# A scheduler's order: evictions of convolved tiles and splits of weight columns given an earlier rank

## The chip, the cores and the metric

The kernel runs on one core of one Trainium2 chip. A core has TensorE (matrix products, written to PSUM banks), VectorE, ScalarE and GpSimd (element-wise work), SyncE (which here only issues DMA transfers), and 16 DMA engines; each engine works through its own queue of instructions, and the engines wait for each other on semaphores. The metric is the device time of one execution in microseconds (us), lower is better.

## The reference

The reference is a two-layer trunk of a diffusion model on 512 latent and 256 context tokens of width 1024, in float32. Layer 0 mixes the tokens with a gated delta rule, layer 1 with retention; each mixer is followed by a feed-forward of width 4096 with squared ReLU. Cut to what matters here:

```python
proj = jnp.concatenate([hc, hl], axis=1) @ w_in            # 768 tokens x 6208 columns
qkv = jnp.concatenate([silu(short_conv(qkv[:, :n_ctx], conv_w)),
                       silu(short_conv(qkv[:, n_ctx:], conv_w))], axis=1)
...
# chunked_linear_attention, for each head and direction, over chunks of tokens
dec = jnp.where(incl, jnp.exp(jnp.where(incl, seg, 0.0)), 0.0)
qk = jnp.einsum('bhncd,bhnsd->bhncs', q, k) * dec
a = jnp.where(strict, jnp.einsum('bhncd,bhnsd->bhncs', k, k) * dec * beta[..., :, None], 0.0)
sol = lax.linalg.triangular_solve(a + jnp.eye(CHUNK, dtype=f32), rhs, ...)
...
def step(s, xs_n):
    un = un - jnp.einsum('bhcd,bhde->bhce', xs_n[5], s)
    o = jnp.einsum('bhcd,bhde->bhce', qd, s) + jnp.einsum('bhcs,bhse->bhce', qkn, un)
    s = s * gt[..., None, None] + jnp.einsum('bhcd,bhce->bhde', kd, un)
```

The short convolution has four taps, along the tokens, for each column on its own. There are 8 query/key heads of 128 and 16 value heads; one query/key head serves two value heads.

## The kernel before, in words

**Products in two parts.** Each float32 product is made as three products of rounded operands: a matrix is split into a rounded part and a remainder (`split`, lines 56 and 57: a ScalarE copy that rounds, then a VectorE subtraction). The normalized tokens lie split and transposed in `xt`. Weights come by DMA into `raw` tiles and are split into `hl` tiles, either as 128 columns of all 1024 rows (`w_cols`, lines 64 to 77; in two halves of 512 rows in layer 0's mixer, in one piece later) or as a block of 256 rows by 512 columns (`w_block`). `raw` has two buffers, `hl` has three in layer 0's mixer and five later.

**Projection tiles.** One tile is 128 columns of the input projection for all 768 tokens. `gemm_pair` makes 24 matmuls for the 512 latent tokens (tile `gl`) and then 24 for the 256 context tokens (`gc`), all at line 91. In layer 0's mixer `self.gc` is `("gl", 2)`, so both draw their PSUM bank from one tag of two buffers.

**Convolved tiles.** There are 32 of them, `conv_tile` (lines 572 to 585): two per pair of value heads for key and query, two for the values. The bank is evicted together with the convolution: ScalarE copies it times the tap c[2] into `acc` (line 579), then VectorE adds the other three taps, one instruction each, each on top of the one before (line 582). A Silu on ScalarE (lines 592, 595, 629) takes `acc` further. The 16 gate tiles z (`z_tile`) are evicted by a Silu at line 442 and stored.

**Eight pairs.** For each pair of value heads p the stages are: `gdn_s1` (key and query tile, norms), `gdn_sv` (two value tiles), `gdn_bt` (24 Relu and 24 Exp on ScalarE for the decay, lines 649 and 657), `gdn_s2` (the decay products: on VectorE a mask at line 673, `qkd` at 679 and `e` at 682, then transposes at 691, a transfer of 32x32 blocks through DRAM, and 30 rounds of elimination at lines 717 and 720), `gdn_iv` (assembling the inverse, products at lines 754 to 797), and twelve `gdn_step`s, six chunks in two directions (products at 847, 848, 865, 875, 886; VectorE at 851, 882, 890, 892; ScalarE at 856, 870, 873). `gdn_y2` (lines 915 to 922) transposes the result. The loop over the pairs in `layer0_mix` weaves the steps of pair p with the inverse of pair p+1, the value tiles of p+1, the key and query tiles of p+2, z tiles, and modulation rows (`mod_rows`, lines 220 to 237).

**What sets the order.** The kernel is written for a scheduler that turns the program into one queue for each engine. It runs the program on a clock of its own and, when an engine is free, gives it that one of the ready instructions that has the lowest rank; the rank is the place in the program. `high_priority(n)` moves the rank of what is written inside it forward by n places. The steps stand in a block with `PRI = 300`, the decay products, the inverse and the output parts in one with `P2 = 400`, the key and query tiles and the decay's exponentials in one with `PS = 250`; the value tiles and z tiles have none. The first two weight columns of each feed-forward and the first of the retention have `WP = 200`. The order thus found is fixed: on the chip each engine takes its queue in that order.

**After the mixer** come the output projection (`out0`), the feed-forward (`ffn`), retention (`layer1_mix`) and the second feed-forward. They use `w_cols` too, for the first matrix of the feed-forwards and for retention's queries and keys; their `proj` uses `w_block`.

## Time and profile before

| | |
|---|---|
| median of 3 runs | 2562.77 us (2562.68 to 2563.67) |
| profiled execution, its own time | 2564.44 us |
| its span, first to last instruction | 2562.7 us |
| mean granted TensorE clock | 0.98 |
| busy: TensorE / weight loads / VectorE / ScalarE / GpSimd | 2431.7 / 2010.7 / 1661.7 / 1074.0 / 163.7 us |
| the evictions at line 579 (ScalarE) and line 582 (VectorE) | 22.0 + 15.3 us and 71.6 + 45.6 us |
| splits of weights, 128x512 halves, lines 56 / 57 | 98 each, 60.6 / 67.4 us |

A row of the groups is read as: line, engine, operation, out<-in, shapes, xcount | busy us, mean ns of one | idle time of that engine just before, and what ended most of it. A row of the waits is: engine and line that waited <- engine and line it waited for: us in total, times, longest. A row of a timeline is: start us, us, engine, line, operation, names, count, and in brackets the engine's idle time before it and what ended that. PE is TensorE's matmul, PEld its weight load, DVE VectorE, ACT ScalarE, POOL GpSimd, SPq the queue of SyncE. The granted clock is the share of full speed that TensorE's throttle allowed.

### The profile page before, as it was taken

How to read it: one execution, taken by the hardware profiler on the slowest of the kernel's cores; microseconds unless marked ns; L12 is line 12 of the kernel's file. 1: busy time of each engine (PE TensorE's matmuls, PEld its weight loads, DVE VectorE, ACT ScalarE, POOL GpSimd, SP SyncE). 2: the span in 40 equal slices, each digit the busy share in tenths (PEclk: the TensorE clock that was granted, in tenths of full speed). 3: DMA queues.
4: the chain of work that ended last, by engine and by line, in shares of the span. 5: the costliest groups of instructions: out<-in, count | busy, mean ns of one | idle time of the engine just before them, and what ended most of it. 6: DMA issues, size and time to landing. Idle time of an engine off the chain costs nothing.

```text
span 2562.7 us, 38997 instructions
## 1 busy us (share of the span) xinstructions
PE 2431.7 (95%) x14879; PEld 2010.7 (78%) x14879; DVE 1661.7 (65%) x3382; ACT 1074.0 (42%) x2357; POOL 163.7 (6%) x248
## 2 busy tenths in 40 slices
PE   8799798998888999999999999999999999999998
PEld 4687686786777787878888888888888887788887
DVE  5568767777776845887876667874353546644446
ACT  5576556565654553253222222653231322532222
POOL 1101111111201110000000000000000000000000
PEclk9899899899999999999999999999999999999999
DMA  6332324333132238354444444243122223433332
GB/s 211 89 96 77 106 51 113 80 105 94 43 109 67 74 113 272 132 165 132 132 144 129 123 130 129 100 135 93 50 84 61 78 66 115 150 97 91 107 91 91
DMA packets 346828, 276.94 MB, mean 108 GB/s; under 512 B 105608, under 2 KB 293488, under 8 KB 346640
## 3 DMA queue, kind: packets, MB, share of 16 engines
q1 hardware_dynamic: 345616, 271.30, 35.2%
q10 hardware_dynamic: 1024, 3.15, 0.5%
q8 instruction: 117, 1.92, 0.3%
q14 instruction: 71, 0.58, 0.1%
HBM read 241.72 MB, written 32.67 MB: 107 GB/s over the span
## 4 chain that ended last, share of the span: by engine, by line
PE 58%; DVE 5%; DMA 2%; ACT 2%; issue 1%; POOL 0%; SPq 0%; POOLq 0%; DVEq 0%; ACTq 0%
PE pn L940 22%; PE gl L91 14%; PE rvp L1257 5%; PE gc L91 3%; PE rl L91 3%; PE rgp L1257 3%; PE pv L1287 3%; PE sc L1265 1%; PE rc L91 1%; PE nps L276 1%; DVE hl L57 0%; DVE ma L199 0%; DMA zt<-zd 0%; PE mps L214 0%; PE uo L865 0%
## 5 line engine op out<-in xcount | busy, mean ns | idle before, releaser
L91 PE MATMUL gl<-xt,hl 128*128 128x512 f32 (+2 forms) x2760 | 704.6, 404 | 53.9 <-DVE acc L582 31.9
L91 PEld LDWEIGHTS gl<-xt,hl 128*128 128x128 f32 x2760 | 517.0, 194 | 161.9 <-issue 27.9
L57 DVE TENSOR_TENSOR hl<-raw,hl 128x1024 fp32r<-128x1024 f32 (+1 forms) x306 | 321.4, 1052 | 231.1 <-ACT hl L56 230.3
L56 ACT ACTIVATE hl<-raw 128x1024 fp32r<-128x1024 f32 (+1 forms) x306 | 280.0, 920 | 409.6 <-PE pn L940 251.9
L940 PE MATMUL pn<-hl,fh 128*128 128x512 f32 x1920 | 444.7, 391 | 2.2 <-DVE fh L1074 1.9
L940 PEld LDWEIGHTS pn<-hl,fh 128*128 128x128 f32 x1920 | 357.3, 188 | 80.0 <-DVE fh L1074 5.0
L91 PE MATMUL gc<-xt,hl 128*128 128x256 f32 x1944 | 273.2, 289 | 8.9 <-DVE acc L582 4.7
L91 PEld LDWEIGHTS gc<-xt,hl 128*128 128x128 f32 x1944 | 253.3, 193 | 19.9 <-ACT zs L442 5.5
L199 DVE SCALAR_TENSOR_TENSOR ma<-mraw,cst,ma 128x256 f32<-128x256 f32 x280 | 123.5, 482 | 40.4 <-DMA mraw<-in_w_mod 38.1
L940 PE MATMUL pn<-hl,yh 128*128 128x512 f32 x576 | 133.8, 392 | 2.5 <-ACT yh L56 1.4
L954 DVE TENSOR_TENSOR facc<-pn,facc 128x512 f32<-128x512 f32 x120 | 82.5, 689 | 81.8 <-PE pn L940 81.5
L1257 PE MATMUL rvp<-hl,xt 128*128 128x512 f32 x576 | 132.8, 389 | 0.0
L940 PEld LDWEIGHTS pn<-hl,yh 128*128 128x128 f32 x576 | 107.2, 188 | 26.8 <-ACT yh L56 2.6
L1257 PEld LDWEIGHTS rvp<-hl,xt 128*128 128x128 f32 x576 | 107.8, 188 | 22.2
L1071 ACT ACTIVATE fr<-gl 128x512 f32<-128x512 f32 x64 | 38.2, 597 | 193.3 <-PE gl L91 190.7
L582 DVE SCALAR_TENSOR_TENSOR acc<-gl,cw,acc 128x511 f32<-128x511 f32 (+1 forms) x96 | 71.6, 746 | 37.9 <-ACT acc L579 37.1
L940 PE MATMUL pn<-hl,ryt 128*128 128x512 f32 x384 | 92.0, 397 | 0.0
L1257 PE MATMUL rgp<-hl,xt 128*128 128x512 f32 x384 | 91.0, 393 | 0.0
L91 PE MATMUL rl<-xt,hl 128*128 128x512 f32 x384 | 89.5, 391 | 0.4 <-DVE hl L57 0.4
L717 DVE TENSOR_TENSOR tmp<-u 112x30 f32<-112x30 f32 (+14 forms) x240 | 81.5, 339 | 9.4 <-POOL u L709 6.2
L940 PEld LDWEIGHTS pn<-hl,ryt 128*128 128x128 f32 x384 | 71.6, 188 | 16.8
L91 PEld LDWEIGHTS rl<-xt,hl 128*128 128x128 f32 x384 | 71.5, 188 | 15.7 <-DVE hl L57 0.9
(282 smaller groups left out, 3347.9 us busy)
## 6 DMA issues: line engine op xcount, KB each, us to landing
raw<-in_w_ff SPq DMA_DIRECT2D x128, 512.0 KB
mraw<-in_w_mod SPq DMA_DIRECT2D x112, 256.0 KB
raw<-in_gdn_w_in SPq DMA_DIRECT2D x96, 256.0 KB
raw<-in_ret_w_in SPq DMA_DIRECT2D x32, 512.0 KB
mraw<-in_w_mod SPq DMA_DIRECT2D x24, 512.0 KB
e<-gd SPq DMA_DIRECT2D x32, 384.0 KB
mraw<-in_w_mod SPq DMA_DIRECT2D x8, 1024.0 KB
raw<-in_gdn_w_out SPq DMA_DIRECT2D x16, 512.0 KB
```

What stands on the lines that cost most here:

```text
L56: nc.scalar.activation(out=hi, in_=src, func=AF.Copy)
L57: nc.vector.tensor_tensor(out=lo, in0=src, in1=hi.bitcast(F32), op=ALU.subtract)
L91: nc.tensor.matmul(ps, lhsT=w(a, k), rhs=xt[:, b, k, t0:t0 + n], start=(k == 0 and i == 0), stop=(k == 7 and i == 2))
L199: eng.scalar_tensor_tensor(out=accs[v], in0=raw[:, k], scalar=c, in1=accs[v], op0=ALU.mult, op1=ALU.add)
L276: nc.tensor.transpose(ps[:, k, :], xn[:, (half * 4 + k) * 128:(half * 4 + k + 1) * 128], self.ident)
L582: nc.vector.scalar_tensor_tensor(out=acc[:, t0 + a:t0 + a + m], in0=ps[:, b:b + m], scalar=c[j], in1=acc[:, t0 + a:t0 + a + m], op0=ALU.mu ...
L717: nc.vector.tensor_tensor(out=t3, in0=u3[:, 0:c, c:c + 1].to_broadcast([112, c, n]), in1=u3[:, c:c + 1, c + 1:32].to_broadcast([112, c, n] ...
L940: m = nc.tensor.matmul(ps, lhsT=lhs(a, k, t), rhs=hls[hf][k // 2][:, b, k % 2], start=(k == 0 and n == 0), stop=(k == 3 and n == 2))
L954: nc.vector.tensor_tensor(out=dst, in0=ps, in1=dst, op=ALU.add)
L1071: nc.scalar.activation(out=r, in_=ps, func=AF.Relu)
L1257: nc.tensor.matmul(ps, lhsT=xt[:, a, kk, t * 128:(t + 1) * 128], rhs=hls[kk // 2][:, b, kk % 2], start=(kk == 0 and n == 0), stop=(kk == 7 ...
L1287: nc.tensor.matmul(pvs[it], lhsT=pts[jt][:, i, it * 128:(it + 1) * 128], rhs=v[:, j, jt], start=(jt == 0 and n == 0), stop=(jt == 5 and n ...
```

## The change

A constant `EV = 500` is added. The split in `w_cols` and the whole loop of evictions in `conv_tile` are put into `high_priority(EV)`. The instructions stay the same, with the same operands; only their rank for the scheduler moves, by 500 places, in addition to that of a block around them. The DMA transfer of the weights and the matmuls keep their rank, as do the evictions of z tiles and the splits in `w_block`.

```diff
@@ -30,6 +30,7 @@
 PRI = 300
 PS = 250
 P2 = 400
+EV = 500
@@ -72,7 +73,8 @@
             hl = self.whl.tile([128, 2, n, 128], F32R, tag="hl", name="hl")
-            self.split(hl[:, 0], hl[:, 1], raw)
+            with self.tc.high_priority(EV):
+                self.split(hl[:, 0], hl[:, 1], raw)
             res.append(hl)
@@ -575,13 +577,14 @@
         acc = prep.tile([128, T], F32, tag="acc", name="acc", bufs=2)
-        for ps, t0, n in segs:
-            nc.scalar.activation(out=acc[:, t0:t0 + n], in_=ps, func=AF.Copy, scale=c[2])
-            for j, a, b in ((0, 2, 0), (1, 1, 0), (3, 0, 1)):
-                m = n - max(a, b)
-                nc.vector.scalar_tensor_tensor(
-                    out=acc[:, t0 + a:t0 + a + m], in0=ps[:, b:b + m], scalar=c[j], in1=acc[:, t0 + a:t0 + a + m],
-                    op0=ALU.mult, op1=ALU.add)
+        with self.tc.high_priority(EV):
+            for ps, t0, n in segs:
+                nc.scalar.activation(out=acc[:, t0:t0 + n], in_=ps, func=AF.Copy, scale=c[2])
+                for j, a, b in ((0, 2, 0), (1, 1, 0), (3, 0, 1)):
+                    m = n - max(a, b)
+                    nc.vector.scalar_tensor_tensor(
+                        out=acc[:, t0 + a:t0 + a + m], in0=ps[:, b:b + m], scalar=c[j], in1=acc[:, t0 + a:t0 + a + m],
+                        op0=ALU.mult, op1=ALU.add)
         return acc
```

## Prediction

> **What bounds the kernel now.** I read the page first, then the busy time by stretch, then who waited for whom on TensorE, and last the timeline around the longest wait.

> ```profile
> span 2562.7 us, 38997 instructions
> PE 2431.7 (95%) x14879; PEld 2010.7 (78%) x14879; DVE 1661.7 (65%) x3382; ACT 1074.0 (42%) x2357; POOL 163.7 (6%) x248
> PEclk9899899899999999999999999999999999999999
> 64.00:960.00 896.00, 798.88 (x7109) 667.37 (x7108) 642.27 (x1639) 520.32 (x1430) 127.74 (x184) 0.95 0.32 87
> 960.00:2562.70 1602.70, 1578.10 (x7511) 1313.86 (x7509) 981.90 (x1660) 520.14 (x871) 24.38 (x44) 1.00 0.37 116
> ```

> The last two rows (stretch, then length, PE, PEld, DVE, ACT, POOL busy, granted clock, DMA share, GB/s) divide the kernel. From 960 us on TensorE is idle for 24.6 of 1602.7 us at full clock: there is next to nothing to win. From 64 to 960 us, the gated delta-rule stage, it is idle for 97.1 us and its granted clock is 0.95. Whatever this change gives must come from those 97.1 us and that clock. VectorE is busy for 642 of the 896 us (0.72), ScalarE for 520.

> Who ended TensorE's idle time between 64 and 960 us (waits in total, times, longest):

> ```profile
> PE gl L91 <- DVE acc L582: 31.9, 11, 9.1
> PE yps L921 <- DVE o L915: 6.7, 8, 1.5
> PE ivps L754 <- DVE v L745: 6.3, 3, 5.9
> PE gl L91 <- ACT zs L442: 5.4, 1, 5.4
> PE gl L91 <- DVE hl L57: 5.4, 3, 3.1
> PE gl L91 <- ACT hl L56: 5.1, 3, 4.2
> PE gc L91 <- DVE acc L582: 4.7, 2, 4.2
> ```

> The evictions of convolved tiles (L582) end 36.6 us in 13 waits, the weight splits (L56, L57) 10.5 us in 6. All the rest, 97.1 − 47.1 = 50.0 us, is waits on the recurrence, its inverse, the z evictions (L442) and small rows. In this stage the latent and the context product of a tile alternate on the two buffers of one PSUM tag, so the next tile's product waits for the eviction of the bank before last. The timeline around the longest wait shows what the eviction stood behind:

> ```profile
> 386.89 7.13 ACT L657 ACTIVATE e<-e,lw 128x128 f32<-128x128 f32 x24
> 389.09 3.03 PE L91 MATMUL gc<-xt,hl 128*128 128x256 f32 x24
> ...
> 396.09 0.67 ACT L579 ACTIVATE acc<-gl,cw 128x512 f32<-128x512 f32 x1
> ...
> 400.24 0.69 DVE L679 TENSOR_TENSOR qkd<-qm,e 128x512 f32<-128x512 f32 x1
> ...
> 400.84 0.75 DVE L582 SCALAR_TENSOR_TENSOR acc<-gl,cw,acc 128x511 f32<-128x511 f32 x1
> ...
> 401.73 4.91 PE L91 MATMUL gl<-xt,hl 128*128 128x512 f32 x14 [9.06 <-DVE acc L582]
> ```

> The tile's bank was full when the context product began at 389.09. ScalarE first ran 24 exponentials of the decay (7.13 us), and the eviction's first step came at 396.09; on VectorE its three further steps then took turns with the decay products (L673, L679, L682). TensorE stood for 9.06 us. This is the order that the change turns round.

> **Evictions.** No instruction is added or removed. Of 32 convolved tiles, 64 ScalarE copies and 192 VectorE steps move. Their rank goes ahead by 500, which is more than the 400 of the decay products and the 300 of the steps; for the key and query tiles it adds to a 250 that they have, for the value tiles there was none. Durations, and those of the decay products:

> ```profile
> L582 DVE SCALAR_TENSOR_TENSOR acc<-gl,cw,acc 128x511 f32<-128x511 f32 (+1 forms) x96 | 71.6, 746 | 37.9 <-ACT acc L579 37.1
> L582 DVE SCALAR_TENSOR_TENSOR acc<-gc,cw,acc 128x255 f32<-128x255 f32 (+1 forms) x96 | 45.6, 475 | 1.3 <-ACT acc L579 0.9
> L679 DVE TENSOR_TENSOR qkd<-qm,e 128x512 f32<-128x512 f32 x48 | 35.3, 735 | 15.8 <-ACT e L657 15.2
> L682 DVE TENSOR_TENSOR e<-kkps,e 128x512 f32<-128x512 f32 x48 | 32.9, 686 | 0.7
> L579 ACT ACTIVATE acc<-gl,cw 128x512 f32<-128x512 f32 x32 | 22.0, 688 | 52.3 <-PE gl L91 52.1
> ```

> Served at once, a latent bank is free after 0.688 + 3 × 0.746 = 2.93 us, while its context product (the row at 389.09) takes 3.03 us: no wait. But the three steps depend on each other, and in the timeline another instruction slips between them; with one of 0.735 us between each the bank is free after 5.13 us, a wait of 2.1 us. I take 2.1 × 0.72, the share of time in which VectorE has something else to do: 1.5 us for each of the 13 waits, 20 us left of 36.6, **17 us gained** (bounds 36.6 − 27.3 = 9.3, and 36.6).

> **Splits.** 98 half-tile splits in this stage, and those of the feed-forward and query/key columns later:

> ```profile
> L57 DVE TENSOR_TENSOR hl<-raw,hl 128x512 fp32r<-128x512 f32 x98 | 67.4, 690 | 32.7 <-ACT hl L56 32.4
> L56 ACT ACTIVATE hl<-raw 128x512 fp32r<-128x512 f32 x98 | 60.6, 629 | 40.8 <-PE gc L91 31.3 <-DMA raw<-in_gdn_w_in 6.9 <-DVE tmp L717 2.3
> 716.87 1.08 SPq L72 DMA_DIRECT2D raw<-in_gdn_w_in  x2
> 721.37 0.61 ACT L56 ACTIVATE hl<-raw 128x512 fp32r<-128x512 f32 x1
> PE gl L91 <- ACT hl L56: 4.1, 1, 4.1
> ```

> The 5.4 us in which the VectorE half was late goes, since what stood ahead of it there were decay transposes and small rows. Of the ScalarE half's 5.1 us, the wait of 4.2 us stays: its weights were requested at 716.87, 4.5 us before the split at 721.37, so the transfer was late and not the rank. The last row is the one wait after 960 us, at the start of the first feed-forward; the split there stood behind norm evictions, its transfer may also have been late, and I take half. 5.4 + 0.9 + 2.0: **8 us** (bounds 0 and 14.6). A split issues no transfer, but it frees the raw buffer for which the next load waits on SP's queue, with the block transfers of the inverse and the recurrence's stores behind it there; earlier splits can only shorten that. Later splits cost nothing in the forecast: a five-buffer ring and up to 24.6 us of idle time in all cover them; if a split took a buffer that an output-projection block needs first, TensorE's feed-forward products would be the cover.

> **Clock.** Six stretches at half clock lie at the waits named so far. The second of them, the wait at which it lies, and the sum of the six:

> ```profile
> 500.50:507.30 6.80, 6.16 (x15) 4.79 (x16) 6.67 (x14) 0.85 (x1) 4.05 (x6) 0.50 0.57 126
> 501.14 5.06 PE L91 MATMUL gl<-xt,hl 128*128 128x512 f32 x11 [2.90 <-DVE acc L582]
> sum 37.40, PE 27.15 PEld 21.00 DVE 30.85 ACT 3.61 POOL 15.11; mean PE 4.52 PEld 3.50 DVE 5.14 ACT 0.60 POOL 2.52
> ```

> 27.15 us of TensorE work ran at half speed, so 13.6 us were lost. I give back the share in which the waits go, 25 of 51.2 us: **7 us** (bounds 0 and 13.6).

> [...]

> **What it costs.** Evictions are 71.6 + 45.6 = 117.2 us of VectorE's 642, 18%, now mostly in front of the recurrence's and the inverse's steps. I let the other 50.0 us of TensorE's waits grow by that share: **9 us**. At best 0, since TensorE has projection products of other tiles to run while a step is late; at worst double, 18. A gain in these waits I exclude, because every instruction they hang on has the same or a later place. What stands behind an early eviction is one step at a time, 0.75 us; behind an early split whose weights are late, the whole ScalarE queue: exponentials, the scaled updates, the next eviction.

> **Sum.** 17 + 8 + 7 − 9 = 23 us. The profiled execution took 2564.4 us, 1.7 above its span and 1.7 above the median of 2562.8; a difference between stages carries over to the median unchanged. 2562.8 − 23 = **2540 us**. With the terms at their ends this case runs from about 2518 to 2556.

> **Rivals.** *Decay products late, slower.* The next pair's first step hangs on its decay products, the block transfer, the inverse and its products. If the evictions of two tiles, 2 × 3 × (0.746 + 0.475) = 7.3 us, go ahead of them in each of seven pairs and each chain moves by all of it, that is 51 us against the 32 gained: 2582 us. It decides against the change from 32 / 7 = 4.6 us per pair. Against it, the same stretch one pair from the end:

> ```profile
> 819.41 0.47 DVE L582 SCALAR_TENSOR_TENSOR acc<-gc,cw,acc 128x255 f32<-128x255 f32 x1
> 819.81 0.67 DVE L682 TENSOR_TENSOR e<-kkps,e 128x512 f32<-128x512 f32 x1
> ```

> The last decay product already ends after the last eviction step, so turning round what lies before moves its end little. For it: evictions that are free earlier let the next tile's come earlier too, into the same stretch. Chance 0.16.

> *The pair chain holds the end, no difference.* The stage's last work, from the chain of waits:

> ```profile
> 945.20 0.63 PE yps L921 x4
> 945.83 0.47 PE gl L91 x2
> 946.30 2.88 PE gc L91 x24
> ```

> The last pair's transposes end at 945.8, the last z tile's product at 949.2. If projection tiles come sooner but the pairs' chain does not, only 3.4 us come off: 2559 us, and idle time moves to the end of the stage. The same would be read if the scheduler's own clock, and not the rank, puts the evictions where they are. Against it: the chain itself starts from key and query tiles that TensorE must first make. Chance 0.13.

> *All of it goes.* Evictions and splits wait for nothing, the clock stays up, and the step chain loses nothing: 36.6 + 14.6 + 13.6 = 65 us, 2498 us; it needs VectorE free at each of the 13 moments. Chance 0.06, with most of it short of that end.

> *Splits hold ScalarE, slower.* Seven of the 98 splits were held by a transfer for 6.9 us together, about 1 us each, and one wait of 4.2 us on TensorE came of it. If all 98 stood at the head of the queue like that, 97 us on ScalarE would become 97 × 4.2 / 6.9 = 59 us on TensorE, 36 us more than the gain: 2599 us. [...] Against this rival stand L56's 31.3 us behind context products: mostly a free buffer, not a transfer, gates a split. Chance 0.05.

> **How the numbers follow.** The forecast has 0.60. A measurement of this kernel can tell about 0.2%, 5 us, from no change. Faster is the forecast and the large gain, 0.66; within 0.2% 0.13; slower 0.16 + 0.05 = 0.21. The range goes from 2512, below the forecast's own end, to 2578, which takes in no difference and most of a slow outcome up to its price; about 0.05 lies below and 0.12 above.

> **What would show it.** Right: in the stage, waits on L582 fall from 36.6 to about 20 us with none above 3, waits on the VectorE half of a split vanish, half-clock stretches after 400 us shrink, ScalarE's copy (L579) stands among the exponentials and not behind them, and after 960 us TensorE is idle for about as long as before. Wrong: if waits on L582 fall but idle time in the stage does not, the cost term was too small, and the rows of L754, L865, L875 and L921 will have grown; if the waits on L582 stay, the rank was not the cause; if L56 waits long on transfers, the last rival holds; if the loss lies after 960 us, it is the ring of split buffers.

## The result, and the profile after

The changed kernel takes 2543.1 us (median of 4 runs, 2540.9 to 2548.3) against 2563.2 us before (4 runs, 2562.7 to 2566.7): a ratio of 0.9925, with an interval from 0.9907 to 0.9943. That is 20 us, four times what a measurement of this kernel can tell from no change. The profiled execution was the slowest of the four, 2548.25 us. In e1 and e12 below one execution each ran at a granted clock of 0.84 and took 7% longer; those two times are left out, and so is e12's profile, which is of one of them. All line numbers after the change are 1 to 3 higher: evictions stand at L582 (ScalarE) and L585 (VectorE), splits at L57 and L58, z evictions at L444. In the kernels of the experiments the same lines stand up to two places off.

The page's first lines, the clock, and the busy time of the two parts of the kernel (stretch, length, PE, PEld, DVE, ACT, POOL busy, granted clock, DMA share, GB/s):

```profile
span 2546.6 us, 38986 instructions
PE 2427.1 (95%) x14879; PEld 2007.0 (79%) x14879; DVE 1656.9 (65%) x3382; ACT 1072.3 (42%) x2357; POOL 162.6 (6%) x248
PEclk9899999999999989999999999999999999999999
60.00:928.60 868.60, 795.15 (x7162) 665.80 (x7160) 637.18 (x1641) 524.16 (x1436) 125.93 (x184) 0.96 0.34 92
960.00:2546.60 1586.60, 1551.68 (x7344) 1290.19 (x7343) 967.01 (x1644) 504.40 (x849) 25.07 (x44) 0.99 0.36 110
```

The mixer's end is best read from the first product of the output projection. It begins at 928.6 us, before at 965.7. The same stretch of before, to compare with the fourth row:

```profile
60.00:965.70 905.70, 808.58 (x7163) 675.85 (x7163) 646.35 (x1644) 526.12 (x1436) 127.74 (x184) 0.95 0.32 88
```

So the mixer is 37.1 us shorter: 13.4 us of them because the same products kept TensorE busy for 795.2 in place of 808.6 us, which is the clock (TensorE's work in stretches at half clock falls from 64.6 to 39.1 us, so 12.8 us less are lost there), and 23.7 us because it is idle for 73.4 in place of 97.1 us. But the span is only 16.1 us shorter (the medians differ by 20.1). From the first output-projection product to the end before took 2562.7 − 965.7 = 1597.0 us, after 2546.6 − 928.6 = 1618.0 us. **21.0 us of the gain are given back after the mixer**, where the forecast had nothing.

Who ended TensorE's idle time from 64 to 960 us:

```profile
PE gl L93 <- ACT zs L444: 13.1, 1, 13.1
PE pn L943 <- ACT hl L57: 12.4, 1, 12.4
PE gl L93 <- ACT hl L57: 6.1, 3, 4.0
PE gl L93 <- DVE acc L585: 6.0, 7, 1.4
...
PE gc L93 <- DVE acc L585: 3.4, 2, 3.1
...
PE gc L93 <- ACT zs L444: 2.2, 2, 1.5
```

The waits on the taps fell from 36.6 us in 13 to 9.4 us in 9. In their place stand two single waits of a dozen us each, which are no evictions of convolved tiles. The first is a z tile's, whose evictions the change left where they were:

```profile
100.50 7.12 ACT L660 ACTIVATE e<-e,lw 128x128 f32<-128x128 f32 x24
107.63 1.28 ACT L444 ACT_TABLE_LOAD   x1
108.92 0.60 ACT L444 ACTIVATE zs<-gl 128x512 f32<-128x512 f32 x1
109.42 0.38 ACT L444 ACTIVATE zs<-gc 128x256 f32<-128x256 f32 x1
109.57 4.78 PE L93 MATMUL gl<-xt,hl 128*128 128x512 f32 x13 [13.11 <-ACT zs L444]
```

This is the picture of the long wait before, with Silu in the eviction's place: 24 exponentials and a table load stand ahead of two evictions of 1 us together. The second lies at the mixer's end:

```profile
913.20 3.03 PE L93 MATMUL gc<-xt,hl 128*128 128x256 f32 x24
921.24 0.38 SPq L83 DMA_DIRECT2D raw<-in_gdn_w_out  x1
927.49 1.06 ACT L57 ACTIVATE hl<-raw 128x1024 fp32r<-128x1024 f32 x1 [1.55 <-DMA raw<-in_gdn_w_out]
928.60 2.06 PE L943 MATMUL pn<-hl,yh 128*128 128x512 f32 x3 [12.37 <-ACT hl L57]
```

Before, the products of two more z tiles ran from 949 us on and covered the loads of the first y, z and weight blocks. Now the projection is used up when the last pair is done, and the loads are bare.

What the change does inside the mixer is seen where the exponentials of a pair meet an eviction:

```profile
649.56 0.69 ACT L582 ACTIVATE acc<-gl,cw 128x512 f32<-128x512 f32 x1 [3.09 <-PE gl L93]
...
650.28 0.75 DVE L585 SCALAR_TENSOR_TENSOR acc<-gl,cw,acc 128x510 f32<-128x510 f32 x1 [0.66 <-ACT acc L582]
...
650.95 0.36 DVE L720 TENSOR_TENSOR tmp<-u 112x198 f32<-112x198 f32 x1
...
651.22 0.75 DVE L585 SCALAR_TENSOR_TENSOR acc<-gl,cw,acc 128x511 f32<-128x511 f32 x1
...
652.15 0.74 DVE L585 SCALAR_TENSOR_TENSOR acc<-gl,cw,acc 128x511 f32<-128x511 f32 x1
...
655.98 0.46 ACT L582 ACTIVATE acc<-gc,cw 128x256 f32<-128x256 f32 x1
...
656.34 3.02 ACT L660 ACTIVATE e<-e,lw 128x128 f32<-128x128 f32 x10
```

The latent bank is free at 652.89, 3.33 us after the copy began, with one step of the elimination (0.36 us) between the taps; the context copy cuts into the run of exponentials. TensorE does not wait here at all.

### The profile page after: what moved, and what is told of

It is laid out like the page before. It is cut to its first block, busy times and chain, and to the rows that moved or that the text cites. A ratio compares the mean times of both kernels' runs of the same rounds, so it can differ in the third digit from the quotient of the medians.

```text
span 2546.6 us, 38986 instructions
## 1 busy us (share of the span) xinstructions
PE 2427.1 (95%) x14879; PEld 2007.0 (79%) x14879; DVE 1656.9 (65%) x3382; ACT 1072.3 (42%) x2357; POOL 162.6 (6%) x248
## 4 chain that ended last, share of the span: by engine, by line
PE 65%; DVE 10%; DMA 4%; ACT 3%; issue 2%; POOL 1%; POOLq 0%; SPq 0%; DVEq 0%; ACTq 0%
PE pn L943 21%; PE gl L93 16%; PE rvp L1260 5%; PE gc L93 5%; PE rl L93 3%; PE rgp L1260 3%; PE pv L1290 3%; DMA mraw<-in_w_mod 1%; DVE hl L58 1%; PE sc L1268 1%; DVE ma L201 1%; PE uo L868 1%; PE uo L889 1%; PE kk L878 1%; PE rc L93 1%
## 5 line engine op out<-in xcount | busy, mean ns | idle before, releaser
L93 PE MATMUL gl<-xt,hl 128*128 128x512 f32 (+2 forms) x2760 | 702.9, 400 | 36.5 <-ACT zs L444 13.1
L93 PEld LDWEIGHTS gl<-xt,hl 128*128 128x128 f32 x2760 | 507.2, 191 | 137.5 <-ACT zs L444 13.6
L58 DVE TENSOR_TENSOR hl<-raw,hl 128x1024 fp32r<-128x1024 f32 (+1 forms) x306 | 322.1, 1055 | 241.8 <-ACT hl L57 234.9
L57 ACT ACTIVATE hl<-raw 128x1024 fp32r<-128x1024 f32 (+1 forms) x306 | 280.8, 920 | 440.8 <-PE pn L943 256.3
L943 PE MATMUL pn<-hl,fh 128*128 128x512 f32 x1920 | 449.9, 393 | 4.3 <-DVE fh L1077 3.6
L93 PE MATMUL gc<-xt,hl 128*128 128x256 f32 x1944 | 278.8, 291 | 7.8 <-DVE acc L585 3.4
L943 PE MATMUL pn<-hl,yh 128*128 128x512 f32 x576 | 135.1, 395 | 13.5 <-ACT hl L57 12.4
L93 PEld LDWEIGHTS rl<-xt,hl 128*128 128x128 f32 x384 | 72.6, 191 | 15.3 <-DVE hl L58 0.3
L1260 PEld LDWEIGHTS rgp<-hl,xt 128*128 128x128 f32 x384 | 71.3, 188 | 14.7
L723 DVE TENSOR_TENSOR u<-u,tmp 112x30 f32<-112x30 f32 (+14 forms) x240 | 80.5, 336 | 2.3
```

The costliest lines, as they stand in the source:

```text
L57: nc.scalar.activation(out=hi, in_=src, func=AF.Copy)
L58: nc.vector.tensor_tensor(out=lo, in0=src, in1=hi.bitcast(F32), op=ALU.subtract)
L93: nc.tensor.matmul(ps, lhsT=w(a, k), rhs=xt[:, b, k, t0:t0 + n], start=(k == 0 and i == 0), stop=(k == 7 and i == 2))
L723: nc.vector.tensor_tensor(out=u3[:, 0:c, c + 1:32], in0=u3[:, 0:c, c + 1:32], in1=t3, op=ALU.subtract)
L943: m = nc.tensor.matmul(ps, lhsT=lhs(a, k, t), rhs=hls[hf][k // 2][:, b, k % 2], start=(k == 0 and n == 0), stop=(k == 3 and n == 2))
L1260: nc.tensor.matmul(ps, lhsT=xt[:, a, kk, t * 128:(t + 1) * 128], rhs=hls[kk // 2][:, b, kk % 2], start=(kk == 0 and n == 0), stop=(kk == 7 ...
```

## The experiments

My theory after the result: the evictions carry the mixer's gain, and the raised splits outside the mixer cost what was lost there. Rivals: the splits carry the gain; or the gain is an accident of the new order, as any small move of ranks would throw it about. Each kernel was timed beside the kernel before on the same chip, which had medians of 2560.0 to 2561.7 us there.

**e1: evictions alone.** `high_priority(EV)` stays in `conv_tile` and is taken out of `w_cols`.

> Only the evictions of convolved tiles get the earlier rank; all splits keep theirs. Theory: the evictions carry most of the 37 us by which the first output-projection product comes sooner (965.7 before, 928.6 changed), and the splits outside the mixer cause the 21 us lost after it. Then that product starts at about 935, the part after it takes 1597 as before, and the time is about 2533 us. Rival A, the splits in the mixer carry the gain: about 2555 to 2563. Rival B, the 21 us lost later do not come from splits (any new order of the mixer leaves them): about 2548 to 2552.

2554.4 us, ratio 0.9974 (0.9960 to 0.9988): a miss for the theory, whose 2533 is 21 us away, at the edge of what rival A gave. The waits from 60 to 960 us:

```profile
PE gl L92 <- ACT hl L57: 15.6, 5, 10.6
PE gl L92 <- DVE acc L584: 11.4, 9, 2.5
PE gc L92 <- DVE acc L584: 10.5, 5, 3.5
```

The evictions' waits fall from 36.6 to 21.9 us, but 10 us of that turn up again as waits on the ScalarE half of the splits, which were 5.1. The mixer ends at 954.0 us, 11.7 earlier and not the 31 of the theory; from there to the end it takes 1597.1 us, as before, which is the theory's other half.

**e2: splits alone.** The reverse: in `w_cols` only, for all stages.

> Only the splits of weight columns get the earlier rank, in the mixer and after it; the evictions keep theirs. Theory: at most 8 us come off in the mixer and about 20 are lost after it: 2570 to 2578 us, slower than before, with the waits on evictions still about 36 us. Rival A, splits carry the gain: 2530 to 2545. Rival B, no loss from splits after the mixer: 2553 to 2558.

2590.2 us, 1.0118 (1.0100 to 1.0137), 12 us above the range expected: the mixer itself is 12.1 us longer, to 977.8.

```profile
PE gl L93 <- DVE acc L584: 25.9, 12, 4.8
PE gc L93 <- ACT zs L444: 11.4, 7, 3.0
...
PE gl L93 <- ACT zs L444: 8.2, 1, 8.2
```

I read it so: with the weights ready earlier, TensorE runs sooner into banks that are still full. The waits on z's rise from 9.6 to 19.6 us; those on the taps fall only from 36.6 to 28.6.

**e3: both, but splits only in the mixer.**

```diff
-            with self.tc.high_priority(EV):
+            with self.tc.high_priority(EV) if parts == 2 else ExitStack():
                 self.split(hl[:, 0], hl[:, 1], raw)
```

> Both parts, but the splits only where a weight column is split in two halves, that is in layer 0's mixer; the feed-forwards and retention keep their splits' rank. Theory: the mixer as in the changed kernel (first output-projection product at about 929), then 1597 us as before: about 2525 us, faster than the changed kernel by about 18. Rival B: within 5 us of the changed kernel, 2538 to 2548.

2525.4 us, 0.986 (0.984 to 0.988), the theory's figure and the fastest of all. The mixer is that of the changed kernel (end at 925.6, taps 7.0 + 3.4 us, the same two long waits), and what follows takes 2522.9 − 925.6 = 1597.3 us, as before the change. Up to 1074 us TensorE, VectorE and ScalarE run the same instructions in the same order as in the changed kernel, so the 3.0 us between the two mixers' ends are what two executions of one order differ by.

**e4: only the later splits** (`parts == 1`) are raised, evictions and the mixer's splits are not.

> Only the splits outside the mixer (one piece, feed-forwards and retention's queries and keys) get the earlier rank; the mixer is that of before. Theory: the mixer ends as before at 965.7, and 14 to 21 us are lost after it, most of them near the norms at the ends of the feed-forwards and beside the modulation parts: 2577 to 2584 us. Rival B: within 5 us of before, 2563.

2578.7 us, 1.0066 (1.0049 to 1.0083): expected. With e3, this shows the loss after the mixer from both sides: by the ratios 17 us come back by leaving those splits alone, and 17 us are lost by raising them alone. The profiled execution, the fastest of its four, divides otherwise: its mixer ends at 961.2 us and not at 965.7, with the same instructions in the same order as before, and the rest takes 1610.1 us, 13.1 more than before. A row that stands in the changed kernel, in e2 and in e4 alike, against that of e3, both for the time after the mixer:

```profile
PE nps L278 <- DVE njunk L274: 7.5, 4, 5.6
```

```profile
PE nps L278 <- DVE njunk L274: 3.0, 4, 1.2
```

The longest of them, in the changed kernel, where the first feed-forward passes into retention:

```profile
1635.05 3.77 PE L93 MATMUL rl<-xt,hl 128*128 128x512 f32 x15
...
1639.72 1.05 ACT L57 ACTIVATE hl<-raw 128x1024 fp32r<-128x1024 f32 x1
...
1640.67 1.05 ACT L262 ACTIVATE njunk<-facc 128x1024 f32<-128x1024 f32 x1
...
1641.06 1.22 DVE L58 TENSOR_TENSOR hl<-raw,hl 128x1024 fp32r<-128x1024 f32 x1
...
1642.20 0.15 DVE L264 TENSOR_SCALAR nr<-nms 128x1 f32<-128x1 f32 x1
...
1644.42 1.97 PE L278 MATMUL nps<-ident,njunk 128*128 128x128 f32 x8 [5.61 <-DVE njunk L274]
```

The same seam before the change:

```profile
1662.90 0.71 PE L91 MATMUL rl<-xt,hl 128*128 128x512 f32 x2
1664.04 5.30 PE L91 MATMUL rl<-xt,hl 128*128 128x512 f32 x22 [0.43 <-DVE hl L57]
1670.54 1.09 PE L276 MATMUL nps<-ident,njunk 128*128 128x128 f32 x8 [1.19 <-DVE njunk L272]
```

On each of the two engines a split of a later weight column runs just before a step of the last token tile's norm, for which TensorE waits. That is the smaller part of this wait: from the feed-forward's last product to the norm's transposes it is 11.0 us in place of 9.6, so the norm itself is 1.5 us later. Most of the rest is that TensorE's own order has 15 of retention's products ahead of the transposes where it had 24, and so less to do meanwhile. The clock halves for 6.8 us from 1642.1 on.

**e5: z evictions raised too,** on top of e3.

```diff
-        for ps, t0, n in self.gemm_pair(w):
-            nc.scalar.activation(out=zs[:, t0:t0 + n], in_=ps, func=AF.Silu)
+        segs = self.gemm_pair(w)
+        with self.tc.high_priority(EV):
+            for ps, t0, n in segs:
+                nc.scalar.activation(out=zs[:, t0:t0 + n], in_=ps, func=AF.Silu)
```

> The version with splits moved in the mixer only, with the two Silu evictions of each z tile moved ahead by 500 as well. In the changed kernel one wait of 13.1 us lies on a z eviction at 109.6 us, behind 24 exponentials, and half clock follows it. Theory (what counts is that no bank eviction stands behind the decay's queue): that wait falls below 3 us, the first steps come some 10 us earlier, and so does the mixer's end: 0.981 of the time before, about 2512 us, 13 below the mixer-only version. Rival (the chain of the first pair sets the start of the steps, z tiles only fill): the wait goes but the first step comes at the same time, and the time stays at 0.986, 2525 us.

2538.1 us, 0.9917 (0.9903 to 0.9932): neither. The wait of 13.1 us is gone, and the kernel is 13 us slower than e3. z's rows fall to 1.1 us at most, the taps' rise from 10.4 to 21.0:

```profile
PE gl L93 <- DVE acc L587: 14.4, 8, 4.1
...
PE gc L93 <- DVE acc L587: 6.6, 3, 2.9
```

The first pair is not earlier but later: its first stores are issued at 234.2 us against 217.3 in e3, the last two from 334.1 against 317.4. GpSimd's first copy of the first pair's decay products begins at 122.5 us in place of 111.5, though what ran before it on GpSimd ends only 2.4 us later (97.8 for 95.4); that the z evictions, now ahead on ScalarE, are what holds the decay up is not shown. A long wait in the list was thus no reserve. Nor is the loss all in the mixer, which ends 9.2 us later than in e3: 7.5 us more lie after it, where from 26 us on TensorE, VectorE and ScalarE run the same order as in e3.

**e6: 150 in place of 500,** on top of e3 (behind the decay products' 400 for the value tiles).

> The mixer-only version with 150 in place of 500. Value tiles then stand 150 ahead, behind the steps' 300 and the decay products' 400; key and query tiles stand at 400 in sum. Theory (an eviction must be ahead of the decay products to be worth anything): waits on the VectorE taps in the mixer come back to over 20 us and the time is 0.992 to 1.000 of the time before, 2541 to 2562 us. Rival (any move forward does, since it only has to pass what was written just before it): 0.986, 2525 us, with waits as at 500.

2566.5 us, 1.0029 (1.0019 to 1.0038), slightly beyond the theory's end and far from the rival's 0.986. Key and query tiles, which stand in a block of 250, come level with the 400 here. The evictions wait longer than before:

```profile
PE gl L93 <- DVE acc L585: 21.5, 13, 4.3
PE gc L93 <- DVE acc L585: 18.9, 7, 3.8
```

**e7 and e8: which engine's queue?** On top of e3, only the copies (L582) or only the three taps (L585) stay in the block.

> The mixer-only version in which of each eviction only ScalarE's copy is moved, the three VectorE taps not. The late splits alone cost 0.0066 of the time and all splits alone 0.0118, so splits in the mixer alone should stand near 1.005, and the evictions bring some 0.019 on top of them, 49 us. Theory A (the bank stood behind ScalarE's exponentials): over half of that is there, 0.991 or less, 2539 us or less. Theory B (it stood behind VectorE's decay products): less than a third, 0.999 or more, 2559 us or more.

> The mirror image: of each eviction the three VectorE taps are moved and ScalarE's copy is not. Theory A (ScalarE's queue held the bank): less than a third of the 49 us, 0.999 or more. Theory B (VectorE's queue): over half, 0.991 or less. If both halves alone give little, a bank is free only when neither queue holds it, and the two parts are not additive for the same reason as evictions and splits.

Copies alone 1.0014 (1.0003 to 1.0024), taps alone 0.9953 (0.9935 to 0.9971). Theory A, ScalarE's exponentials, falls: with the copies alone nothing is gained on the kernel before. Theory B's half is about there for the taps, short of its 0.991. Neither alone comes near 0.986. What each adds to splits raised in the mixer alone is not known: their 1.005 is a difference of two ratios, and that kernel was not run.

**e9, e10, e11: 420, 1000 and 10 in place of 500,** on top of e3, to see how far the order scatters.

> The mixer-only version (0.986 with 500) with 420 in place of 500: still ahead of the decay products' 400. Theory (what counts is to pass the decay products): like 500, 0.984 to 0.990 of the time before, 2519 to 2534 us. Rival (the order came out well by chance, and any small change of a rank throws the pairs' periods about by several us, as single moves did with 0.995 to 1.003): anywhere between 0.990 and 1.000.

> The mixer-only version with 1000 in place of 500. Theory: a plateau, 0.984 to 0.990, since an eviction that is at the head of its queue gains nothing by more. Rival (chance of the order): between 0.990 and 1.000.

> The mixer-only version with 10 in place of 500, a move that passes next to nothing: a measure of how far the order and the time move without a purpose. Theory: within 0.3% of the time before, 2552 to 2568 us, with waits on the taps in the mixer above 25 us. Rival (scatter of the order as large as the effects discussed): off by 0.5% or more to either side, which would make single moves of 0.3 to 0.5% unreadable.

0.9970 (0.9957 to 0.9982), 0.9925 (0.9909 to 0.9942), 1.0071 (1.0056 to 1.0086). All three went to the rival: there is no plateau at 0.986, and a move of 10 places, which passes next to nothing, costs 0.7%. The rows of the slowest of the three, e11, whose evictions wait longest of all versions:

```profile
PE gl L93 <- DVE acc L585: 27.2, 11, 7.0
PE gc L93 <- DVE acc L585: 20.6, 8, 4.7
```

All versions but e12 by their waits on the taps (the two rows `gl` and `gc` of the waits added), with the start of the first output-projection product and the rest of the span. These three are of one profiled execution each, up to 7 us from the median of its kernel; the ratio is of medians:

| | taps, us | mixer's end, us | rest, us | ratio |
|---|---|---|---|---|
| changed kernel | 9.4 | 928.6 | 1618.0 | 0.9925 |
| e3, 500, splits in the mixer | 10.4 | 925.6 | 1597.3 | 0.9860 |
| e9, 420 | 13.4 | 941.3 | 1605.2 | 0.9970 |
| e10, 1000 | 13.8 | 939.5 | 1606.6 | 0.9925 |
| e5, z too | 21.0 | 934.8 | 1604.8 | 0.9917 |
| e1, evictions alone | 21.9 | 954.0 | 1597.1 | 0.9974 |
| e7, copies | 22.5 | 971.4 | 1596.1 | 1.0014 |
| e2, splits alone | 28.6 | 977.8 | 1617.3 | 1.0118 |
| e8, taps | 29.8 | 943.0 | 1600.6 | 0.9953 |
| e4, later splits alone | 35.5 | 961.2 | 1610.1 | 1.0066 |
| before | 36.6 | 965.7 | 1597.0 | 1 |
| e6, 150 | 40.4 | 968.9 | 1594.8 | 1.0029 |
| e11, 10 | 47.8 | 980.7 | 1599.7 | 1.0071 |

Three things stand out of the scatter. With both parts moved in the mixer, the three ranks from 420 up end it 24 to 40 us earlier, and 10 places end it 15 us later; the 3 us of 150 places are no more than two executions of one order differ by. So what decides stands between 150 and 420 places. That can be the decay products' 400, but the steps' 300 and the exponentials' 250 lie there too, and no run separates them. Within the three above, the same idea ends the mixer anywhere from 925.6 to 941.3 us, 16 us apart. And the waits on the taps alone do not set the mixer's end: e8 has 29.8 us of them and ends it at 943.0, e7 has 22.5 and ends it at 971.4.

The last stages show what a single execution can tell. In the ten versions that leave the later splits alone, TensorE, VectorE and ScalarE run the same order from 28 us after the mixer's end at the latest, and yet they take 1594.8 to 1606.6 us, 1600 on average. With the later splits raised it is another order, the same in the changed kernel, e2 and e4, and takes 1610.1 to 1618.0 us, 1615 on average.

**e12: the stages' first splits left in place,** on top of the changed kernel: the first four columns of each feed-forward and the first head's queries and keys.

```diff
-                        w = self.w_cols(self.i["w_ff1"][l][:, c0:c0 + 128], 1)
+                        w = self.w_cols(self.i["w_ff1"][l][:, c0:c0 + 128], 1, b > 0)
...
-                w = self.w_cols(load, 1)
+                w = self.w_cols(load, 1, col % 1024 > 0)
```

> The changed kernel, with the splits left in place only where a new stage begins: those of the first four columns of each feed-forward and of the first head's queries and keys; all later splits stay 500 ahead. Theory (the loss after the mixer comes from splits that stand ahead of the norm's statistics, where TensorE waits 5.6 us and the clock then halves): most of the 18 us comes back, 0.986 to 0.988 of the time before, 2525 to 2530 us. Rival (each raised split inside the stages holds ScalarE and VectorE in front of the squares and the evictions): stays at 0.992, 2541 us.

2534.7 us, 0.9887 (0.9870 to 0.9903), between the two theories. Of the 0.0065 between the changed kernel and e3, 0.0038 come back, so by medians rather more than half of the loss lies at the junctions. That the rest lies with splits inside the stages is only what remains: the intervals of e12 and e3 overlap a little, and by what e9 to e11 show, a difference of this size between two single orders is weak evidence.

## Why the prediction was right, and where it was not

The direction and the size were right, 20 us for a forecast of 23. The composition was not. From the two profiled executions, which are 16.1 us apart:

| term | forecast, us | measured, us |
|---|---|---|
| waits on evictions | 17 | 27.2 |
| waits on splits in the mixer | 6 | 3.9 |
| clock in the mixer | 7 | 13.4 |
| other waits in the mixer | −9 | −7.4 |
| split at the first feed-forward's start | 2 | 0 |
| everything else after the mixer | 0 | −21.0 |

**Evictions.** Each of the 13 waits was to keep 1.5 us. There are 9 left with 1.0 us on average, and the longest is 3.1 us, just above the bound of 3 that was set. The picture behind the term holds: copy among the exponentials, taps with one short step between them, TensorE not waiting. What fell is the way the sum was made, part by part. Raised alone, the evictions end the mixer 11.7 us earlier, the splits alone 12.1 us later, and both together 37.1 us earlier. A projection tile needs its weights and a free bank at once; whichever is not moved becomes the wait. That reading fits e1 (splits' waits up by 10 us) and e2 (the taps' waits still 28.6 us, z's up by 10), but why the pair of them gives as much as it does is argued, not shown.

**Splits.** The VectorE half was to be on time, and is: 5.4 became 0.5 us. The ScalarE half was to keep its 4.2 us wait and kept one of 4.0; its sum was to fall from 5.1 to 4.2 us and rose to 6.1, so the term gave 3.9 us for 6. At the start of the first feed-forward I took half of 4.1 us, and the row is unchanged at 4.1, since its rank did not move that split in ScalarE's queue: it starts at 1070.5 us right behind a norm's evictions, in the same place as in e3, where it is not raised. A late transfer does not show there, as ScalarE has no idle time ahead of this split.

**Clock.** This term was sized on too few stretches. I gave back the share in which the waits go, 7 of the 13.6 us lost in the six stretches named. But between 60 us and the mixer's end there were 14 stretches at half clock, with 64.6 us of TensorE's work, and after the change there are 11 with 39.1 us; TensorE's busy time for the same products fell by 13.4. What sets off the half clock is not shown: of the 11 stretches that are left, five follow 3.4 us in which TensorE was busy throughout.

**Cost.** The other 50.0 us of waits were to grow by 18%. As a sum they did nearly that, by 15% to 57.4, and not for the reason given. The recurrence, the inverse and the small rows shrank: without z and the output projection they were 50.0 − 9.6 = 40.4 us and are 57.4 − 15.3 − 12.4 = 29.7. What grew is z's evictions (9.6 to 15.3 us) and the bare loads at the mixer's end (12.4 us). The first I had counted among waits that would grow a little; e5 shows that to remove it is no gain. The second is what the rival "the pair chain holds the end" described, idle time that moves to the end of the stage. But that rival's premise was wrong, since the pairs' chain does come sooner: the last pair's transposes begin at 910.0 us and not at 945.2. Its price of 3.4 us was misread too, as two more z tiles' products ran before the change from 949.0 us to the mixer's end. The wait is there with 11.8 to 13.0 us in e3, e5, e8 and e9, with 5 to 7 us in e7 and e10, and not before the change or in e11. Whether earlier loads would help was not tried.

**After the mixer.** This step failed: "Later splits cost nothing in the forecast: a five-buffer ring and up to 24.6 us of idle time in all cover them". I asked whether buffers would be short, and not what the splits would pass in their queues. A later split is 1.06 us on ScalarE and 1.22 on VectorE, and raised by 500 places it goes ahead of norms, modulation and evictions of the stage that is ending. TensorE was busy for nearly all of that part (1572.4 of 1597.0 us before the change), so there was no gain to be had against that loss. Its price is shown by e3 and e4, about 17 us by the ratios. How it comes about is shown less well: at the one seam looked at, the norm is 1.5 us later behind the splits, and most of what else the wait of 5.6 us has grown by comes of a changed order of TensorE's own products. By stretches of the two profiles, the first feed-forward is 9.9 us longer (560.0 for 550.1), retention's start 6.1 (118.0 for 111.9), the second feed-forward 6.0 (373.3 for 367.3):

```profile
1112.80:1662.90 550.10, 545.62 (x2813) 465.93 (x2812) 405.67 (x806) 183.84 (x332) 4.33 (x9) 1.00 0.43 132
1662.90:1774.80 111.90, 110.28 (x516) 90.69 (x515) 72.09 (x142) 47.55 (x88) 4.64 (x10) 1.00 0.34 104
```

```profile
1075.00:1635.00 560.00, 550.49 (x2814) 467.62 (x2813) 405.27 (x801) 182.59 (x330) 4.97 (x9) 0.99 0.42 130
1635.00:1753.00 118.00, 112.39 (x517) 92.75 (x516) 74.84 (x148) 48.61 (x91) 4.65 (x10) 0.97 0.33 100
```

Both columns move, idle time (4.5 to 9.5 us in the first stretch) and the busy time at a lower clock; over the whole rest they account for 10.4 and 10.6 us. The last sentence of the prediction would have sent me to the ring of split buffers, and none of the waits of TensorE that grew there leads to it.

**The rivals.** Decay products that come too late did not show: the waits on the recurrence and the inverse fell. Splits that hold ScalarE for want of weights did not either; the splits that did harm had theirs, and stood in front of others.

**How much was luck.** e9 and e10 are the same change in the mixer with another number, and end it 24.4 and 26.2 us earlier, which is the forecast's 23 more nearly than the changed kernel's 37.1. That the mixer gave 14 us more than reckoned and the rest took 21 is two errors that cancelled.

## What to carry to other kernels

To move a rank is worth trying on what frees a bank, together with what feeds the same product, and only in the stage where the profile shows these waits; here the same line in three other stages gave back about half of the gain. When one number decides the order of a long list-scheduled queue, run its neighbours: between 420 and 1000 the time moved by 1.1% with nothing else changed, so a difference of half a per cent between two single orders says little about the idea behind them. A profile is one execution: the same order took 12 us more or less for the last 1600. The longest wait in a list is not a reserve until something is shown to hang on it.

## What was unexpected of the hardware

TensorE's clock halved in a stretch in which it had no wait. In the kernel before, two stretches beside each other, and the products at the seam:

```profile
460.00:466.30 6.30, 6.30 (x45) 5.56 (x42) 2.99 (x9) 2.95 (x6) 0.00 (x0) 1.00 0.73 182
466.30:473.10 6.80, 6.80 (x38) 5.02 (x39) 3.04 (x10) 4.37 (x10) 2.96 (x7) 0.50 0.17 32
```

```profile
463.08 1.40 PE L604 MATMUL ssps<-ones,sq 128*128 128x1 f32 x12
...
465.52 1.91 PE L604 MATMUL ssps<-ones,sq 128*128 128x1 f32 x12
```

Before most other drops TensorE was idle for a part of the time. Cut into pieces of 3.41 us by the clock's own changes, the kernel before has 717 pieces at full clock, and 17 of them are followed by half clock. In 16 of the 17 TensorE is busy for 0.56 of the piece or less, but only in six is it idle for 0.99 of it or more. Of the 700 others only four are busy for 0.56 or less, and none for less than 0.49. The seventeenth is the one that ends at 466.3. Its products have 1556 columns in all, against 7680 in the median of the 700, but three pieces that were busy throughout, with 1585 to 2067 columns, kept the full clock, so the columns alone do not tell the drops apart.
